# Low parts of a layer's weights kept in DRAM for its second pass, and one subtraction moved from GpSimd to VectorE

## The chip, the cores and the metric

One core of one Trainium2 chip. The metric is the device time of one execution in microseconds (us), the median of three runs. TensorE (PE, with its weight loads as PEld), VectorE (DVE), ScalarE (ACT), GpSimd (POOL) and SyncE (SP, which issues the DMAs here) each run their own in-order queue of instructions and wait for each other by semaphores.

## The reference, cut to what matters

Two layers over 1024 tokens of width 1024. Layer 0 is gated linear attention; layer 1 is sparse attention in which an indexer picks up to 256 keys for each query. What the change touches is in layer 1:

```
h = x @ w_in                       # q: 16 heads x 128, z: 2048, k, v and the indexer's inputs
logits = q . k_sel * ATTN_SCALE    # masked to the chosen keys
probs  = softmax(logits)
o      = probs . v_sel
y      = (o * silu(z)) @ w_out     # 2048 -> 1024
x = layer_norm(ALPHA * x + y);  x = x + (p[i] @ ple_w[i]) * sigmoid(x @ ple_gate_w[i])
```

All of it is float32. The kernel computes each product of two float32 matrices as three matmuls of a reduced type (float32r): each operand a is split into a high part hi = round(a) and a low part lo = a - hi, and hi*hi + hi*lo + lo*hi are summed in PSUM.

## The kernel before

**Two halves.** Each layer runs over 512 tokens, then over the other 512. In layer 1 the first half lies at about 1065 to 1560 us of the span, the second at 1560 to 2134 us, each with a tail (the norm and the gate) behind its 16 heads. Every weight of 128 x 1024 is loaded from DRAM and split anew in each half.

**Weights.** The class `Weights` walks a fixed list `seq` of keys. For each one it loads 512 KB into `wst` (two buffers) by the SP queue, and then makes the parts in four steps: two ACT copies give the halves of `whi` (line 162), two DVE subtractions the halves of `wlo` (line 164); each part has four buffers. `pace` lets a step go when 1.15 us of the kernel's own estimate of TensorE's time have passed, and at most two weights ahead of the one taken; `take` makes what is missing. A `wst` buffer is loaded again when the steps that read it are done. The keys of layer 1 are `dq` (16 blocks of q), `dz` (16 of z), `do` (16 of the output projection), then `p` and `t` for the tail.

**Heads.** `slots()` lays out 17 stretches ("slots"), each with two to four units of weights (q, z or output blocks, 24 matmuls for each weight), and between their matmuls the work of the attention is put in by due times in the same estimate. For head h, `attend` makes:
- A: scores S by PE, minimum and mask into `P` by DVE (line 1357), exp by ACT (line 1377), reciprocal by DVE (line 1381);
- `scaled` and `turned`: the probabilities into `sq` by ACT (line 1365; POOL in the first half, line 1367), and 32 x 32 transposes by DVE (line 1373);
- `store` and `load`: `sq` to DRAM in four DMAs of 256 KB for each group of four key blocks, and back in another order as `PT`, 1 MB at a time (lines 1395 and 1405): one load for a head in the first half, two in the second;
- `parts(g)`: the split of `PT`. ACT copies the high part `ph` (line 1422); 0.8 us of the estimate later a subtraction leaves the low part in `PT` (line 1420). There are three groups g for a head in the first half and seven in the second;
- `pv(g)`: o += vT hi, lo times ph and vT hi times the low part, on PE (tiles `o<-ph,vT`, `o<-PT,vT`), between the matmuls of the weights.

In line 1420 the engine is chosen by half and group: DVE for the even groups (0, 2, 4, 6) of the second half, POOL for its odd groups (1, 3, 5) and for all groups of the first half.

The order of instructions on each engine is that in which this Python code emits them; `manual_schedule` keeps it.

Of the kernel before, what the change touches and what calls it, by code (L numbers as in the profile page):

```python
# [10 lines left out]
F32 = mybir.dt.float32  # L11
# [36 lines left out]
class Flow:  # L48


    def __init__(self, nc):
        self.pe = nc.tensor
        self.now, self.n, self.heap, self.pacers = 0.0, 0, [], []
# [18 lines left out]
    def chain(self, *steps):  # L72

        (_, first), rest = steps[0], steps[1:]
        first()
        if rest:
            self.after(rest[0][0], lambda: self.chain((0, rest[0][1]), *rest[1:]))
# [30 lines left out]
    def pace(self):  # L108
        late = []
        while self.heap and self.heap[0][0] <= self.now:  # L110
            self.one(late)
        self.put_back(late)
        for p in self.pacers:
            p(self.now)
# [23 lines left out]
class Weights:  # L138


    def __init__(self, nc, pool, seq):
        self.nc, self.pool, self.seq = nc, pool, seq
        self.nd = self.ns = self.nu = self.part = 0
        self.due = 0.0
        self.staged, self.parts = {}, {}

    def pace(self, now):
        if now >= self.due and self.step():
# [2 lines left out]
    def step(self):  # L151
        if self.ns >= min(self.nu + 2, len(self.seq)):
            return False
        n, i = self.ns, self.part
        if i == 0:
            self.loads(n + 1)
            self.parts[n] = tuple(self.pool.tile([128, 1024], F32R, tag=t, name=t, bufs=4) for t in ("whi", "wlo"))
        st = self.staged[n]
        hi, lo = self.parts[n]
        c = slice((i % 2) * 512, (i % 2) * 512 + 512)  # L160
        if i < 2:
            self.nc.scalar.activation(hi[:, c], st[:, c], AF.Copy)  # L162
        else:
            self.nc.vector.tensor_sub(lo[:, c], st[:, c], hi[:, c].bitcast(F32))  # L164
        self.part = (i + 1) % 4
        if i == 3:
            self.staged.pop(n)
            self.ns += 1
            self.loads(self.ns + 2)
        return True  # L170
# [42 lines left out]
def trunk_kernel(ctx, tc, x_tok, x_T, p_T, pos, freq, g_q, g_k, g_v, g_z, g_a, g_a2, g_ba, g_gn, g_o,  # L213
                 d_q, d_k, d_v, d_z, d_qi, d_ki, d_o, ln_gb, ple_c, gate_c, out):
    nc = tc.nc
    act, dve, pool = nc.scalar, nc.vector, nc.gpsimd
# [4 lines left out]
    wp = ctx.enter_context(tc.tile_pool(name="wp", bufs=1))  # L221
    xp = ctx.enter_context(tc.tile_pool(name="xp", bufs=1))
    dp = ctx.enter_context(tc.tile_pool(name="dp", bufs=1, space=bass.MemoryType.DRAM))
# [10 lines left out]
    seq = []  # L234
# [7 lines left out]
    def tail_keys(layer):  # L242
        return ([(("p", layer, c), ple_c[layer, c]) for c in range(2)]
                + [(("t", layer, b), gate_c[layer, b]) for b in range(NK)])
# [46 lines left out]
    for half in range(NH):  # L291
# [1 line left out]
            for u in units:  # L293
                seq += unit_keys(u)
        seq += tail_keys(1)
    W = Weights(nc, wp, seq)
    bg, bg2 = Background(), Background()
    fl.pacers += [W.pace, bg.pace, bg2.pace]

# [40 lines left out]
    def pbank():  # L340
        return psum[0].tile([128, 512], F32, tag="pb", name="pb", bufs=psum[1])
# [15 lines left out]
    class XT:  # L357


        def __init__(self):  # L360
            self.t = [None] * NK
# [12 lines left out]
    def fm_block(key, X, evac):  # L374

        hi, lo = W.take(key)
        ps = pbank()
# [119 lines left out]
    def v_phase(u, X):  # L497
        h = u["h"]
        banks = [pbank(), pbank()] + [pp.tile([128, 512], F32, tag="U", name="U", bufs=2) for _ in range(2)]
        for c in range(4):  # L500
            hi, lo = W.take(("v", h, c))
            for t in range(4):
# [188 lines left out]
    def accumulate(parts, U, y, ch, rs=None, norm=None):  # L691

        nb = 2 * len(parts)
        for t in range(4):
            ps = pbank()
            n = 0
            for b in range(nb):
                uh, ul = U(t, b)
                hi, lo = parts[b // 2]
                ws = slice((b % 2) * 512, (b % 2) * 512 + 512)  # L700
                for l, r in ((uh, hi), (uh, lo), (ul, hi)):
                    mm(ps, l, r[:, ws], n == 0, n == 3 * nb - 1)
                    n += 1
                if b < nb - 1:
                    yield
            ys = y[:, t, ch * 512:ch * 512 + 512]
            if rs is not None:
                dve.scalar_tensor_tensor(ys, ps, rs[:, t:t + 1], ys, op0=OP.mult, op1=OP.add)
            else:
                dve.tensor_add(ys, ps, ys)  # L710
            if norm is not None:
                norm(t)
            yield

    def out_phase(u, y, norm=None):
# [4 lines left out]
        for ch in range(2):  # L720
            parts = [W.take(("o", u["h"], ch, 0)), W.take(("o", u["h"], ch, 1))]
            for i, _ in enumerate(accumulate(parts, U, y, ch, u["rs"], norm if ch else None)):
# [39 lines left out]
    def tail(layer, Pt, y, y_done, final, tp, xps, x_alloc, tmp):  # L762
# [15 lines left out]
        for c in range(2):  # L778
            hi, lo = W.take(("p", layer, c))
            for b in range(4):  # L780
# [164 lines left out]
    def index_steps(T, sc, res, kih, kil, ipsum, rtile):  # L945

        n = (T + 1) * 128
        t = T % 4

        def step(i, a, e):  # L950
            def f():
                fl.req(res["q"][i] is not None, "w" in res, "ki" in res)
                e2 = max(e, 256)
                ps = ipsum()
                q = res["q"][i][:, t * 128:t * 128 + 128]
                mm(ps[:, :e2], q, kih[:, a:a + e2], True, False)
                mm(ps[:, :e2], q, kil[:, a:a + e2], False, True)
                r = rtile()
                w = res["w"][:, t, i:i + 1]
                d = sc[:, a:a + e]  # L960

                def add():
                    if i == 0:
                        dve.tensor_scalar(d, r[:, :e], w, None, op0=OP.mult)
                    else:
                        dve.scalar_tensor_tensor(d, r[:, :e], w, d, op0=OP.mult, op1=OP.add)
                    res["n"] = res.get("n", 0) + 1
                    if i == 7 and a + e == n:
                        dve.copy_predicated(sc[:, n - 128:], fmask, negs)
                chain((0, lambda: act.activation(r[:, :e], ps[:, :e], AF.Relu)), (0.8, add))  # L970
            return f

        return fl.ordered([step(i, a, e) for i in range(8) for a, e in cuts(n)])
# [101 lines left out]
    def start_half(half):  # L1075
# [7 lines left out]
        def load(k, n):  # L1083
            nc.sync.dma_start(raw[:, k:k + n], x_T[k:k + n, :, hs].rearrange("k p t -> p k t"))

        def feed():
            load(0, 1)
            W.loads(W.ns + 1)
            load(1, 1)
# [34 lines left out]
    for half in range(NH):  # L1124
# [19 lines left out]
        for h, u in enumerate(units):  # L1144
# [23 lines left out]
            bulk, n = [], 0  # L1168
# [156 lines left out]
    def attend(st, h, half, ap, sq):  # L1325
# [10 lines left out]
        def get(*keys):  # L1336
            fl.req(*(k in st for k in keys))
            return [st[k] for k in keys]
# [70 lines left out]
        def parts(g):  # L1409
            def f():  # L1410
                (j, t0), n = groups[g][0], len(groups[g])
                PT, = get(("PT", h, j // 4))
                fl.req(st["sp"] - st["pv"] < 3)
                st["sp"] += 1
                lo = PT.rearrange("p a (j c) -> p j a c", c=128)[:, j % 4:j % 4 + n, :, 32 * t0:]
                ph = ap.tile([128, HT], F32R, tag="ph", name="ph", bufs=3)
                hi = ph[:, :n * (HT - 128 * t0)].rearrange("p (j a c) -> p j a c", j=n, a=4)

                def second():
                    (dve if half and g % 2 == 0 else pool).tensor_sub(lo, lo.bitcast(F32), hi.bitcast(F32))  # L1420
                    st["parts", h, g] = hi, lo
                chain((0, lambda: act.activation(hi, lo.bitcast(F32), AF.Copy)), (0.8, second))  # L1422
            return f
# [32 lines left out]
        n = range(len(groups))  # L1456
# [75 lines left out]
    for half in range(NH):  # L1532
# [11 lines left out]
        for h, units in enumerate(plan, -1):  # L1544
            start = st["slot"] = fl.now
            dur = sum(len(u[1]) if u[0] == "o" else 1 for u in units) * B + core * (1.0 if h >= 0 else 0.5)
            if h >= 0:
                _, parts, pvs, _, loads = S[h]
# [4 lines left out]
            if h < 15:  # L1553
                first, _, _, stores, loads = S[h + 1]
# [98 lines left out]
```

## Time and profile before

| | |
|---|---|
| median of 3 runs | 2134.95 us (2131.09 to 2135.63) |
| profiled execution | 2135.7 us |
| its span in the trace | 2133.9 us |
| PE busy | 1999.2 us, 94% of the span |
| DVE, ACT, POOL busy | 1539.9 us (72%), 1153.4 us (54%), 326.0 us (15%) |
| TensorE's granted clock, mean | 0.984 of full speed |
| DMA queue q1 | 284.37 MB, 41.5% of 16 engines' span |

Busy time is the union of an engine's instructions; idle time in front of an instruction is put down to the one that released it. The chain of work that ended last follows the last instruction back, at each step to what released it or to the instruction ahead of it on its engine.

### The profile page before, as it was taken

How to read it: one execution, taken by the hardware profiler on the slowest of the kernel's cores; microseconds unless marked ns; L12 is line 12 of the kernel's file. 1: busy time of each engine (PE TensorE's matmuls, PEld its weight loads, DVE VectorE, ACT ScalarE, POOL GpSimd, SP SyncE). 2: the span in 40 equal slices, each digit the busy share in tenths (PEclk: the TensorE clock that was granted, in tenths of full speed). 3: DMA queues.
4: the chain of work that ended last, by engine and by line, in shares of the span. 5: the costliest groups of instructions: out<-in, count | busy, mean ns of one | idle time of the engine just before them, and what ended most of it. 6: DMA issues, size and time to landing. Idle time of an engine off the chain costs nothing.

```text
span 2133.9 us, 26298 instructions
## 1 busy us (share of the span) xinstructions
PE 1999.2 (94%) x8984; PEld 1619.7 (76%) x8984; DVE 1539.9 (72%) x3187; ACT 1153.4 (54%) x2105; POOL 326.0 (15%) x355
## 2 busy tenths in 40 slices
PE   8999999999999999999989899998898889998979
PEld 6788888888788888888867777776686677776767
DVE  5665555676767767667699888786986777777764
ACT  5563535344566353535466677775446655555533
POOL 0100000001011000001012443332112111112110
PEclk9999999999999999999999999999999999999989
DMA  4422222234332222222434555554347665656532
GB/s 141 159 81 79 88 71 89 70 100 143 134 124 70 80 81 83 85 80 84 148 129 151 181 178 169 168 167 153 113 142 231 201 200 195 207 179 212 181 121 97
DMA packets 94197, 286.03 MB, mean 134 GB/s; under 512 B 11120, under 2 KB 11760, under 8 KB 87920
## 3 DMA queue, kind: packets, MB, share of 16 engines
q1 hardware_dynamic: 94064, 284.37, 41.5%
q8 instruction: 70, 1.15, 0.2%
q14 instruction: 63, 0.52, 0.1%
HBM read 220.56 MB, written 63.77 MB: 133 GB/s over the span
## 4 chain that ended last, share of the span: by engine, by line
PE 57%; DVE 20%; ACT 8%; DMA 5%; issue 5%; SPq 1%; POOL 1%; DVEq 0%; POOLq 0%; ACTq 0%
PE pb L58 43%; PE o L58 6%; PE U L58 6%; DVE wlo L164 4%; DVE P L1357 2%; DVE sq L1373 2%; DMA PT<-sqd 1%; PE S L58 1%; DVE rt L853 1%; ACT sq L1365 1%; ACT P L1377 1%; POOL PT L1420 1%; SPq L1395 1%; DMA sqd<-sq 1%; DVE tk L988 1%
## 5 line engine op out<-in xcount | busy, mean ns | idle before, releaser
L58 PE MATMUL pb<-x,whi 128*128 128x512 f32 x2272 | 711.7, 394 | 5.1 <-ACT whi L162 2.4
L58 PEld LDWEIGHTS pb<-x,whi 128*128 128x128 f32 x2272 | 420.1, 189 | 83.6 <-ACT whi L162 3.2
L58 PE MATMUL pb<-x,wlo 128*128 128x512 f32 x1136 | 445.4, 392 | 0.5 <-DVE wlo L164 0.5
L164 DVE TENSOR_TENSOR wlo<-wst,whi 128x512 fp32r<-128x512 f32 x556 | 390.8, 719 | 64.7 <-ACT whi L162 64.3
L162 ACT ACTIVATE whi<-wst 128x512 fp32r<-128x512 f32 x556 | 327.3, 621 | 137.0 <-PE pb L58 28.7
L58 PE MATMUL pb<-whi,u 128*128 128x512 f32 x1024 | 346.0, 398 | 9.5 <-ACT u L352 5.0
L58 PEld LDWEIGHTS pb<-x,wlo 128*128 128x128 f32 x1136 | 214.3, 189 | 48.5 <-DVE wlo L164 2.2
L58 PEld LDWEIGHTS pb<-whi,u 128*128 128x128 f32 x1024 | 195.3, 191 | 50.1 <-ACT u L352 5.8
L58 PE MATMUL pb<-wlo,u 128*128 128x512 f32 x512 | 202.3, 395 | 0.0
L1420 POOL TENSOR_TENSOR PT<-PT,ph 128x512 fp32r<-128x512 f32 (+1 forms) x96 | 131.0, 1371 | 250.3 <-ACT ph L1422 233.1
L58 PE MATMUL o<-ph,vT 128*128 128x512 f32 (+2 forms) x384 | 110.4, 374 | 23.6 <-ACT ph L1422 23.6
L1377 ACT ACTIVATE P<-P,ms 128x128 f32<-128x128 f32 (+7 forms) x128 | 98.6, 770 | 59.3 <-DVE ms L1357 51.5
L58 PE MATMUL S<-kT,q 128*128 128x512 f32 (+2 forms) x576 | 123.1, 344 | 6.3 <-DVE q L344 3.3
L58 PE MATMUL o<-PT,vT 128*128 128x512 f32 x192 | 77.9, 406 | 51.7 <-POOL PT L1420 27.4
L58 PEld LDWEIGHTS S<-kT,q 128*128 128x128 f32 x576 | 100.1, 188 | 26.3 <-DVE q L344 6.1
L58 PEld LDWEIGHTS pb<-wlo,u 128*128 128x128 f32 x512 | 98.0, 191 | 18.4
L1422 ACT ACTIVATE ph<-PT 128x512 fp32r<-128x512 f32 (+1 forms) x160 | 92.6, 598 | 34.2 <-DMA PT<-sqd 11.3
L58 PEld LDWEIGHTS o<-ph,vT 128*128 128x128 f32 x384 | 73.8, 204 | 45.6 <-ACT ph L1422 33.5
L661 ACT ACTIVATE junk<-o 128x512 bf16<-128x512 f32 x32 | 19.1, 597 | 161.1 <-DVE ot L659 151.7
L1373 DVE STREAM_TRANSPOSE sq<-sq 128x128 f32<-128x128 f32 (+7 forms) x128 | 97.0, 764 | 11.0 <-ACT sq L1365 7.2
L1030 ACT ACTIVATE tk<-sc,tki 128x768 f16<-128x768 f32 (+2 forms) x90 | 92.8, 1031 | 22.4 <-DVE tki L1039 21.5
L58 PEld LDWEIGHTS o<-PT,vT 128*128 128x128 f32 x192 | 39.1, 204 | 79.3 <-POOL PT L1420 41.7
(308 smaller groups left out, 3444.9 us busy)
## 6 DMA issues: line engine op xcount, KB each, us to landing
sqd<-sq SPq DMA_DIRECT2D x192, 256.0 KB, 4.4
PT<-sqd SPq DMA_DIRECT2D x48, 1024.0 KB, 6.8
wst<-in_g_v SPq DMA_DIRECT2D x32, 512.0 KB, 3.3
wst<-in_g_z SPq DMA_DIRECT2D x32, 512.0 KB, 3.4
wst<-in_g_o SPq DMA_DIRECT2D x32, 512.0 KB, 3.3
wst<-in_gate_c SPq DMA_DIRECT2D x32, 512.0 KB, 3.5
wst<-in_d_q SPq DMA_DIRECT2D x32, 512.0 KB, 4.6
wst<-in_d_z SPq DMA_DIRECT2D x32, 512.0 KB, 3.5
```

Source lines behind the costliest of these rows:

```text
L58: self.pe.matmul(out, lhsT, rhs, start=start, stop=stop)
L162: self.nc.scalar.activation(hi[:, c], st[:, c], AF.Copy)
L164: self.nc.vector.tensor_sub(lo[:, c], st[:, c], hi[:, c].bitcast(F32))
L853: dve.stream_shuffle(a, x, swap)
L988: dve.tensor_scalar(junk()[:, :n], scs[j], thr_ap, None, op0=op, op1=OP.add, accum_out=cnt[:, j:j + 1])
L1030: act.activation(junk()[:, :n], scs[j], AF.Sign, bias=cand[:, j:j + 1].bitcast(F32), accum_out=cnt[:, j:j + 1])
L1357: dve.tensor_tensor_reduce(P[:, a:a + e], ps[:, :e], bias_t[T][:, a:a + e], op0=OP.add, op1=OP.min, scale=-ATTN_SCALE, scalar=lim, accum_o ...
L1365: act.activation(to, rows, AF.Copy, scale=sm)
L1373: dve.transpose(x, x)
L1377: act.activation(P, P, AF.Exp, scale=-1.0, bias=mx, accum_out=sm)
L1420: (dve if half and g % 2 == 0 else pool).tensor_sub(lo, lo.bitcast(F32), hi.bitcast(F32))
L1422: chain((0, lambda: act.activation(hi, lo.bitcast(F32), AF.Copy)), (0.8, second))
```

## The change

In the first half of layer 1, the low part of each `dq`, `dz` and `do` weight is made as before, and is then also stored to a DRAM tensor `wlos` of its own (512 KB, issued by SP at the second step of the next weight). In the second half these 48 weights have two steps in place of four: the first ACT copy goes out together with a DMA load of the low part from `wlos` into `wlo`, then the second ACT copy; no DVE subtraction. A `wst` buffer is then free after the second copy. The `p` and `t` weights and all of layer 0 are as before.

In line 1420, POOL's odd groups of the second half go to DVE; the first half stays on POOL.

```
-    def __init__(self, nc, pool, seq):
+    def __init__(self, nc, pool, seq, kept, dram):
...
+        self.kept, self.dram, self.low, self.late = kept, dram, {}, None
...
+        key = self.seq[n][0]
...
+        stored = key in self.low
         if i < 2:
             self.nc.scalar.activation(hi[:, c], st[:, c], AF.Copy)
+            if stored and i == 0:
+                self.nc.sync.dma_start(lo.bitcast(F32), self.low[key])
         else:
             self.nc.vector.tensor_sub(lo[:, c], st[:, c], hi[:, c].bitcast(F32))
-        self.part = (i + 1) % 4
-        if i == 3:
+        if i == 1 and self.late:
+            late, self.late = self.late, None
+            self.low[late[0]] = self.dram.tile([128, 1024], F32, name="wlos")
+            self.nc.sync.dma_start(self.low[late[0]], late[1].bitcast(F32))
+        last = i == (1 if stored else 3)
+        self.part = 0 if last else i + 1
+        if last:
+            if key in self.kept and not stored:
+                self.late = key, lo
             self.staged.pop(n)
...
+    kept = {key for key, _ in seq if key[0] in ("dq", "dz", "do")}
+    W = Weights(nc, wp, seq, kept, dp)
...
-                    (dve if half and g % 2 == 0 else pool).tensor_sub(lo, lo.bitcast(F32), hi.bitcast(F32))
+                    (dve if half else pool).tensor_sub(lo, lo.bitcast(F32), hi.bitcast(F32))
```

## Rows read from the trace of the kernel before

**Rows 1.** The page: busy time, and the chain that ended last.
```profile
PE 1999.2 (94%) x8984; PEld 1619.7 (76%) x8984; DVE 1539.9 (72%) x3187; ACT 1153.4 (54%) x2105; POOL 326.0 (15%) x355
...
PE 57%; DVE 20%; ACT 8%; DMA 5%; issue 5%; SPq 1%; POOL 1%; DVEq 0%; POOLq 0%; ACTq 0%
```

**Rows 2.** Busy time by stretch; at each row's end PE clock, DMA share, GB/s.
```profile
1065.00:1470.00 405.00, 371.19 (x1697) 300.17 (x1695) 340.31 (x818) 282.61 (x600) 130.37 (x129) 0.98 0.51 162
...
1560.00:2045.00 485.00, 435.24 (x1928) 347.14 (x1927) 358.00 (x759) 275.83 (x471) 90.30 (x63) 0.97 0.62 196
```

**Rows 3.** Waits of PE, 1560 to 2045 us: total us, times, longest.
```profile
PE o L58 <- DVE PT L1420: 23.7, 21, 2.3
PE o L58 <- ACT ph L1422: 13.3, 10, 4.2
PE o L58 <- POOL PT L1420: 11.2, 12, 2.5
```

**Rows 4.** The chain that ended last, 1560 to 2045 us: shares by line.
```profile
by line: PE pb L58 16.3%; PE o L58 9.5%; issue 7.9%; DVE P L1357 7.2%; DMA PT<-sqd 6.4%; ACT sq L1365 5.7%; DVE wlo L164 5.5%; DVE sq L1373 4.9%; ACT P L1377 3.9%; SPq L1395 3.4%; PE S L58 3.3%; DMA sqd<-sq 3.3%; DVE PT L1420 2.6%; ACT ph L
```

**Rows 5.** Groups by form, 1560 to 2045 us: busy, mean ns, idle before.
```profile
L164 DVE TENSOR_TENSOR wlo<-wst,whi 128x512 fp32r<-128x512 f32 x98 | 71.8, 745 | 6.6 <-ACT whi L162 6.6
...
L1420 POOL TENSOR_TENSOR PT<-PT,ph 128x512 fp32r<-128x512 f32 x31 | 48.9, 1583 | 161.5 <-ACT ph L1422 161.5
...
L1420 DVE TENSOR_TENSOR PT<-PT,ph 128x512 fp32r<-128x512 f32 x62 | 45.4, 739 | 20.2 <-ACT ph L1422 19.9
```

**Rows 6.** Timeline of PE, four waits: start us, us, last the wait.
```profile
1640.77 0.73 PE L58 MATMUL o<-ph,vT 128*128 128x512 f32 x2 [1.06 <-ACT ph L1422]
...
1674.03 0.51 PE L58 MATMUL o<-PT,vT 128*128 128x512 f32 x1 [1.82 <-DVE PT L1420]
...
1731.12 0.50 PE L58 MATMUL o<-PT,vT 128*128 128x512 f32 x1 [2.48 <-POOL PT L1420]
...
1754.85 0.50 PE L58 MATMUL o<-PT,vT 128*128 128x512 f32 x1 [1.33 <-DVE PT L1420]
```

**Rows 7.** Timeline of DVE, and of POOL, ahead of three of these waits.
```profile
1669.98 1.07 DVE L164 TENSOR_TENSOR wlo<-wst,whi 128x512 fp32r<-128x512 f32 x1
...
1672.13 0.64 DVE L164 TENSOR_TENSOR wlo<-wst,whi 128x512 fp32r<-128x512 f32 x1
...
1673.30 1.27 DVE L1420 TENSOR_TENSOR PT<-PT,ph 128x512 fp32r<-128x512 f32 x2
...
1728.06 0.67 DVE L344 TENSOR_TENSOR q<-qf,q 128x512 fp32r<-128x512 f32 x1
...
1727.65 4.38 POOL L1420 TENSOR_TENSOR PT<-PT,ph 128x512 fp32r<-128x512 f32 x2 [3.59 <-ACT ph L1422]
...
1752.49 0.65 DVE L164 TENSOR_TENSOR wlo<-wst,whi 128x512 fp32r<-128x512 f32 x1
```

**Rows 8.** A piece of the chain that ended last: start us, us, what.
```profile
1631.41 0.60 DVE wlo L164
```

**Rows 9.** Busy time by stretch behind a wait; PE clock third from the end.
```profile
1849.00:1852.00 3.00, 3.00 (x8) 2.33 (x9) 0.00 (x0) 0.45 (x1) 0.75 (x1) 0.50 0.93 251
```

**Rows 10.** Waits of the DMA queue (SP), 1560 to 2045 us.
```profile
SPq L175 <- DVE wlo L164: 166.1, 28, 12.6
```

**Rows 11.** DMA issues, 1560 to 2045 us: count, KB each, us to landing.
```profile
PT<-sqd SPq DMA_DIRECT2D x32, 1024.0 KB, 7.0
wst<-in_d_z SPq DMA_DIRECT2D x16, 512.0 KB, 4.1
```

**Rows 12.** Waits of ACT, 1560 to 2045 us.
```profile
ACT whi L162 <- PE pb L58: 13.3, 3, 5.0
...
ACT ph L1422 <- DMA PT<-sqd: 8.9, 1, 8.9
```

**Rows 13.** Issue times of weight loads, 1560 to 2045 us: ns minimum, median, maximum.
```profile
L175 SPq DMA_DIRECT2D wst<-in_d_z x16: 328/333/487, 1562.8 to 1986.7; - x16
```

**Rows 14.** Timeline of ACT at the first half's last head.
```profile
1475.05 1.04 ACT L1422 ACTIVATE ph<-PT 128x512 fp32r<-128x512 f32 x2 [2.42 <-DMA PT<-sqd]
```

More of the change, by code (lines that the diff above doesn't have):

```diff
@@ L295, in trunk_kernel @@
         seq += tail_keys(1)
-    W = Weights(nc, wp, seq)
+    kept = {key for key, _ in seq if key[0] in ("dq", "dz", "do")}
+    W = Weights(nc, wp, seq, kept, dp)
     bg, bg2 = Background(), Background()
```

## The prediction

> **What bounds the kernel now.** The page first: TensorE (PE) is busy for 94% of the span, no other engine for more than 72%, and the chain that ended last lies on PE for 57% and on VectorE (DVE) for 20% [rows 1]. So time is won only where PE stands still or runs at its lower clock. The table by stretch says where: of the 485 us of layer 1's second half (1560 to 2045) PE is busy for 435.2, of the first half's 405 us for 371.2; DVE is busy for 74% of the one and 84% of the other [rows 2]. The changed subtractions run in the second half alone. There PE's waits are 48.2 us, and all three rows belong to the split of the probabilities: 23.7 us for a DVE subtraction of `PT`, 13.3 us for ACT's copy `ph`, 11.2 us for a POOL subtraction [rows 3]. PE waits nowhere for a `wlo`. Yet the chain shows that the 98 `wlo` subtractions are not harmless: 5.5% of 485 us, 26.7 us, of what ended last is `wlo` [rows 4]. They stand in DVE's queue ahead of what PE waits for. To know which, each wait has to be looked at.
>
> **The change part by part.** All sums are made on the profiled execution, 2135.7 us (span 2133.9, 1.8 around it); the median of the runs shown is 2134.95, 0.75 lower.
>
> *DVE's load, second half.* 48 weights lose 2 subtractions each: 96 of the 98 at 745 ns, 71.5 us of DVE. Three odd groups for each of 16 heads come over: 48 at the 739 ns that DVE's own take, 35.5 us (a bound from above, as a third of them have 384 columns and not 512) [rows 5]. Net 36 us of 358 leave DVE. That is load and not time; the time is what PE's waits lose:
>
> (a) Three waits of 1.8 us (heads 1 to 3), one of which is shown at 1674.03 [rows 6]. The subtraction began at 1673.30, and in the 3.3 us ahead of it two `wlo` took 1.07 and 0.64 us [rows 7]. Without them it comes 1.7 us sooner; one subtraction from POOL (0.7) enters the queue. I take 1.0 us each: 3.0.
>
> (b) Three waits of 2.48 us for POOL (heads 4, 8, 12), one at 1731.12 [rows 6]. POOL was slow there: it began at 1727.65, and its two subtractions together took 4.38 us [rows 7], the first until PE's start at 1731.1, 3.4 us, where the mean is 1.58 [rows 5]. On DVE the same work would stand about behind the `q` of 1728.06 [rows 7], and be done at 1728.06 + 0.6 + 0.7, about 1729.3. That is 1.8 us sooner, and at most 2.5; I take 2.0 each: 6.0.
>
> (c) Five waits of 1.33 or 1.44 us for the first group (heads 5, 6, 9, 10, 13), one at 1754.85 [rows 6], each with one `wlo` of 0.6 us close ahead, as at 1752.49 [rows 7]: 0.6 each, 3.0.
>
> (d) Six waits of 1.0 to 1.1 us for `ph` (heads 1, 2, 3, 5, 9, 13), one at 1640.77 [rows 6]. ACT is late there since the minimum, exp and transposes of the next head were late, and the chain through them has a `wlo` of 0.60 us, as at 1631.41 [rows 8]: 0.6 each, 3.6.
>
> (e) POOL's other nine waits, 11.2 - 7.4 = 3.8 us: between nothing (DVE's subtraction is 0.74 us against 1.58, but stands in a longer queue) and all of it. I take 1.0, near the lower end, since DVE's 62 cost PE 0.38 us each now (23.7/62) and POOL's 46 only 0.24 (11.2/46) [rows 3, 5].
>
> (f) The clock. Behind some of these waits the granted clock is 0.50, the 1.2 GHz level, as from 1849 to 1852 [rows 9]; such a stretch of 3.4 us does 1.7 us less. Five follow the waits of (a) and (b). Bounds 0 and 8.5; the waits shrink and don't all go, so I take one: 1.7.
>
> Together 18.3 us. The heads' first waits with no `wlo` ahead stay.
>
> *The stores, first half.* DVE and ACT do what they did. SP issues 48 more DMAs at 0.33 us, 16 us in 405 [rows 13]. A store waits for the same `wlo` for which SP already stands before the next `wst` load, which goes out ahead of it [rows 10] (shown for the second half), so it adds no wait of its own. Behind it on SP are `sqd` stores, `PT` loads and `wst` loads. Its bytes count: 512 KB take about 7.0 - 4.1 = 2.9 us (a load of 1024 KB against one of 512 KB) [rows 11]. What hides that is that `PT` mostly lands before its use. Where it doesn't, PE pays: ACT waited 2.42 us for the last head's [rows 14] and 8.9 us for one in the second half [rows 12]. Bounds: nothing, and 2.9 us for each of 16 loads, 46. I take three loads at half of 2.9, nearer nothing, since two waits among 48 loads are all that the trace has: 4.4 us.
>
> *The loads, second half.* 48 loads of 25 MB raise 196 GB/s to about 248, and the DMA share from 0.62 to about 0.78 [rows 2]. A load goes out at a weight's first step, up to two weights ahead. It waits until PE has let go of the buffer, as the ACT copy beside it does; ACT waited for that three times, 13.3 us in all [rows 12]. SP could wait as long, with `sqd`, `PT` and `wst` DMAs behind it. Bounds 0 and 13.3; nothing taken, as ACT's wait cost PE none. Landing takes 4.1 us [rows 11], and until PE takes the weight there are one or two others to go, 10 us each (48 in 485): hidden. If SP stands for 9 us first, it isn't. `wst` buffers come free sooner, which hurts nobody.
>
> Sum: 18.3 - 4.4 = 13.9 us won, 2135.7 - 13.9 = 2121.8: 2122.
>
> **Rivals.** *The wait only moves.* DVE takes its queue in order, and each of its `PT` subtractions now stands for 0.32 us waiting for ACT's `ph` (19.9/62) [rows 5]; 48 more make 15 us in which DVE does nothing. If the odd groups then cost PE what the even ones cost, 0.38 us, that is 18.2 us for POOL's 11.2, a loss of 7.0. Of (a) to (f) then stay (a), (c) and (d), 9.6, less 4.4 for the stores: 1.8 us lost, 2137.5. For it: DVE waits cost more for each subtraction than POOL's. Against: those are costly because of the `wlo` ahead.
>
> *The way through DRAM becomes the bound (slower).* `PT` loads, SP's stores and the landing of `sqd` are 6.4 + 3.4 + 3.3 = 13.1% of the chain in the second half, 63.5 us [rows 4]. If their 47 us of transfer stretch as the DMA share does (0.78/0.62), that is 12 us more; with SP's 48 issues of 0.33 us on the same path 16 us, and 5 us in the first half: 33 lost against 18.3 won, 15 more: 2150. It decides where a `PT` lands later than it is needed; ACT's single wait of 8.9 us [rows 12] says that most have some us to spare, and the 16 us count only if each issue falls on the path. The Trainium skill, "DMA: Bandwidth & Descriptors", section "Queues, rings and completion order", has the rule that would do this: each DMA engine takes a ring's descriptors in order, so a `PT` load behind a 512 KB transfer waits it out. By that rule each collision costs the 2.9 us taken above, and 2122 becomes this rival's 2150 if nearly every load collides; no row here shows such a collision by itself.
>
> *The low parts come late.* If SP is held and PE waits for `wlo` at the double output units, 2 to 3 us in some four heads: 10 us, 2132. For it only SP's longest wait, 12.6 us [rows 10].
>
> **How the numbers follow.** Less than 0.2% (4.3 us) is about what a measurement of this kernel can't tell from no change. Forecast and its variants that win over 4.3 us: 0.68. The wait moves or the gain is eaten up, within 4.3 us: 0.17. Transfers on the path, slower: 0.15 (late low parts count half in the one and half in the other). The likeliest is 2122. The lower end: all `wlo` on the chain (26.7) and POOL's waits (11.2), less 48 x 0.20 us (DVE's `PT` on the chain, 2.6% of 485 over 62 [rows 4]) = 28, and two clock stretches, 3.4: 31.7 won, 2104. The upper end: a third of the way from 2135.7 to the slow rival, 2140. That leaves 1 in 10 below and 1 in 10 above.
>
> **What would show it.** In the second half: 2 `wlo` on DVE beside 48 loads of `wlo` from DRAM; some 110 `PT` subtractions on DVE at 0.68 to 0.74 us and none on POOL; DVE busy some 36 us less; PE's waits for `PT` down from 34.9 to about 22, for `ph` from 13.3 to about 10, the three waits of 2.48 us gone; clock at 0.97 or 0.98. In the first half: 48 stores, DVE unchanged, the stretch up to 5 us longer. It would be wrong if PE waits for DVE's `PT` exceed 35 us, if waits for `PT<-sqd` pass 20 us, or if PE's row shows a DMA into `wlo`.

## The result, and the profile after

| | before | after |
|---|---|---|
| median | 2135.29 us (4 runs, 2131.09 to 2137.63) | 2104.22 us (4 runs, 2099.89 to 2106.36) |
| profiled execution, its span | 2135.7, 2133.9 us | 2106.36, 2104.1 us |
| ratio to before, 95% interval | | 0.9854 (0.9831 to 0.9877) |

The change makes the kernel 31 us faster, 1.46%. The forecast was 13.9 us, 2122; the measured time stands at the lower end of the range. The direction and the place were right; the forecast gain was less than half of the measured one.

Where the time went shows in one instruction that each half has once, the clearing of `sq` by GpSimd (count, then ns minimum, median and maximum, then the first and the last start). Before:

```profile
L1539 POOL MEMSET sq<- x2: 1798/2665/3532, 1080.2 to 1567.1; 128x2048 f32 x1, 128x4096 f32 x1
```

After:

```profile
L1553 POOL MEMSET sq<- x2: 1797/2660/3524, 1078.6 to 1565.6; 128x2048 f32 x1, 128x4096 f32 x1
```

Layer 1's second half begins 1.5 us sooner; the span ends 29.8 us sooner. So 28.3 us were won behind the start of the second half, and the first half, with its 48 stores, lost nothing in this execution.

The busy time by stretch, after (columns as in [rows 2]):

```profile
1065.00:1470.00 405.00, 370.58 (x1693) 299.71 (x1691) 338.04 (x818) 283.47 (x602) 132.60 (x129) 0.98 0.70 220
...
1560.00:2013.00 453.00, 429.92 (x1918) 346.53 (x1918) 316.47 (x709) 275.60 (x470) 24.11 (x17) 0.97 0.77 264
```

In the second half VectorE is busy for 316.5 us where it was 358.0: 41.5 less, 36 were forecast. The DMA share is 0.77 (0.78 was forecast). The granted clock is the same 0.97 as in [rows 2], but as the mean of two parts that moved apart. Heads 1 to 3 and the heads behind them, before:

```profile
1640.00:1706.00 66.00, 55.43 (x232) 42.95 (x233) 47.46 (x97) 39.67 (x69) 15.23 (x12) 0.92 0.63 194
1706.00:2045.00 339.00, 305.74 (x1366) 244.44 (x1365) 249.17 (x533) 190.08 (x325) 62.62 (x44) 0.99 0.61 195
```

After:

```profile
1637.00:1703.00 66.00, 58.73 (x241) 46.44 (x241) 45.78 (x97) 40.58 (x70) 2.84 (x3) 0.87 0.74 243
1703.00:2013.00 310.00, 299.17 (x1355) 241.06 (x1354) 219.76 (x499) 188.89 (x323) 12.86 (x10) 1.00 0.77 265
```

In heads 1 to 3 the clock fell from 0.92 to 0.87, behind them it rose from 0.99 to 1.00. PE's waits from 1560 to 2013 us, which answer to [rows 3]:

```profile
PE o L58 <- DVE PT L1434: 14.0, 15, 1.8
PE o L58 <- ACT ph L1436: 5.4, 5, 3.7
PE pb L58 <- DMA wlo<-wlos: 3.2, 1, 3.2
```

48.2 us of waits have become 22.6: 25.6 won, where the forecast's items (a) to (e) came to 16.6. The wait for a low part from DRAM, a rival's mechanism and one of the forecast's own signs of being wrong, is there once. VectorE's groups, after:

```profile
L1434 DVE TENSOR_TENSOR PT<-PT,ph 128x512 fp32r<-128x512 f32 (+1 forms) x108 | 68.3, 654 | 23.5 <-ACT ph L1436 23.5
```

All 108 subtractions of `PT` in the stretch are on VectorE. The mean is over two shapes; those of 128 x 512 alone took 671 ns, where VectorE's took 739 before, beside POOL's [rows 5].

The DMAs of the second half (count, KB each, us to landing), after, against [rows 11]:

```profile
PT<-sqd SPq DMA_DIRECT2D x31, 1024.0 KB, 7.6
wlo<-wlos SPq DMA_DIRECT2D x47, 512.0 KB, 7.8
```

`PT` lands 0.6 us later than before; the new loads take 7.8 us, nearly twice what a `wst` load of z took (4.1).

### The profile page after: what moved, and what is told of

It reads as the page before. It is cut to its first block, busy times and chain, and to the rows that moved or that the text cites. A ratio compares the mean times of both kernels' runs of the same rounds, so it can differ in the third digit from the quotient of the medians.

```text
span 2104.1 us, 26226 instructions
## 1 busy us (share of the span) xinstructions
PE 1998.5 (95%) x8984; PEld 1622.8 (77%) x8984; DVE 1496.1 (71%) x3139; ACT 1153.6 (55%) x2105; POOL 258.6 (12%) x307
## 3 DMA queue, kind: packets, MB, share of 16 engines
q8 instruction: 70, 1.15, 0.2%
## 4 chain that ended last, share of the span: by engine, by line
PE 65%; DVE 14%; ACT 8%; DMA 6%; issue 5%; POOL 1%; SPq 1%; DVEq 0%; POOLq 0%; ACTq 0%
PE pb L58 48%; PE o L58 7%; PE U L58 6%; DVE wlo L170 2%; PE S L58 2%; ACT sq L1379 2%; DVE P L1371 1%; DMA wlo<-wlos 1%; ACT P L1391 1%; DVE sq L1387 1%; DMA PT<-sqd 1%; DVE rt L867 1%; DVE sc L980 1%; DVE tk L1002 1%; SPq L1409 1%
## 5 line engine op out<-in xcount | busy, mean ns | idle before, releaser
L170 DVE TENSOR_TENSOR wlo<-wst,whi 128x512 fp32r<-128x512 f32 x460 | 317.0, 706 | 57.1 <-ACT whi L166 55.4
L1436 ACT ACTIVATE ph<-PT 128x512 fp32r<-128x512 f32 (+1 forms) x160 | 93.8, 599 | 44.4 <-DMA PT<-sqd 16.6
L58 PE MATMUL pb<-whi,x 128*128 128x512 f32 x256 | 89.2, 408 | 9.5 <-ACT whi L166 6.2
L866 POOL TENSOR_TENSOR rt<-qf,tab 32x512 f32<-32x512 f32 x32 | 41.8, 1306 | 439.0 <-ACT qf L1288 433.1
```

Of the source, the lines that this page charges most:

```text
L58: self.pe.matmul(out, lhsT, rhs, start=start, stop=stop)
L866: pool.tensor_mul(b, x, c)
```

## The experiments

All ran beside runs of the kernel before on the same chip; each ratio is to those.

| run | what it is | median us | ratio to before, 95% interval |
|---|---|---|---|
| e1_weights_only | low parts from DRAM, odd groups on POOL | 2099.52 | 0.9841 (0.9824 to 0.9858) |
| e2_engine_only | weights as before, all groups on VectorE | 2125.36 | 0.9965 (0.9952 to 0.9978) |
| e3_stores_only | stores, never read | 2136.51 | 1.0011 (0.9999 to 1.0023) |
| e4_more_traffic | changed kernel, 48 more copies | 2104.70 | 0.9861 (0.9841 to 0.9880) |
| e8_time_back | e1, with a transpose for each removed subtraction | 2124.07 | 0.9948 (0.9934 to 0.9963) |
| e9_sub_back | e1, with a subtraction for each removed one | 2137.73 | 1.0015 (1.0006 to 1.0025) |
| e5_low_by_pool | low parts made by POOL, no DRAM | 2126.56 | 0.9959 (0.9945 to 0.9972) |
| e6_pool_early_heads | changed kernel, odd groups of heads 0 to 3 on POOL | 2100.34 | 0.9843 (0.9829 to 0.9857) |
| e7_pool_late_heads | changed kernel, odd groups of heads 4 to 15 on POOL | 2102.91 | 0.9853 (0.9838 to 0.9868) |
| e10_last_by_dve | e1, last three output weights made again | 2099.96 | 0.9837 (0.9822 to 0.9853) |

**The two parts of the change, each alone.** First the weights alone, against the changed kernel:

```
-                    (dve if half else pool).tensor_sub(lo, lo.bitcast(F32), hi.bitcast(F32))
+                    (dve if half and g % 2 == 0 else pool).tensor_sub(lo, lo.bitcast(F32), hi.bitcast(F32))
```

> Low parts from DRAM in the second half; the odd groups stay on POOL. Theory Q (VectorE's queue: the time won is mostly that of the weights' subtractions standing ahead of what TensorE waits for): 16 to 22 us faster than before, about 2116; VectorE is busy some 75 us less in the second half, TensorE's waits for VectorE's PT fall from 23.7 to under 12 us, waits for POOL's PT stay at 8 to 11. Theory P (GpSimd: its subtractions are slow and slow VectorE's): under 12 us faster, 2124 or more, and the waits for POOL's PT stay at 11 us.

34 us won: by the medians more than the whole change, though the two intervals overlap. Both theories were too low, and both expected more waits for POOL. PE's waits, 1560 to 2006 us, weights alone:

```profile
PE o L58 <- DVE PT L1434: 10.0, 13, 1.3
PE o L58 <- ACT ph L1436: 5.3, 5, 3.6
PE pb L58 <- DMA wlo<-wlos: 4.5, 3, 3.4
PE o L58 <- POOL PT L1434: 4.2, 8, 0.6
```

The waits for POOL fell from 11.2 to 4.2 us, the longest from 2.5 to 0.6, though POOL does what it did before. The forecast's item (b), 6 us, was booked to the move to VectorE; the weights alone bring it. VectorE's own subtractions of `PT` did not get shorter beside POOL's: 62 of them take 807 ns, where they took 739 [rows 5].

```profile
L1434 DVE TENSOR_TENSOR PT<-PT,ph 128x512 fp32r<-128x512 f32 x62 | 49.4, 807 | 22.4 <-ACT ph L1436 22.2
```

The other part alone, in the kernel before:

```
-                    (dve if half and g % 2 == 0 else pool).tensor_sub(lo, lo.bitcast(F32), hi.bitcast(F32))
+                    (dve if half else pool).tensor_sub(lo, lo.bitcast(F32), hi.bitcast(F32))
```

> All groups of the second half on VectorE, the weights made as before. Theory Q: VectorE is 36 us busier, its queue longer; the 11.2 us of POOL waits turn into VectorE waits: between 3 us faster and 10 us slower than before, 2132 to 2145. Theory P: at least 8 us faster, 2127 or less.

0.35% faster, 7.5 us: theory P's side for this one. PE's waits and VectorE's two subtractions, 1560 to 2036 us:

```profile
PE o L58 <- DVE PT L1420: 30.8, 25, 2.4
PE o L58 <- ACT ph L1422: 12.4, 8, 4.2
```

```profile
L164 DVE TENSOR_TENSOR wlo<-wst,whi 128x512 fp32r<-128x512 f32 x96 | 63.8, 676 | 6.2 <-ACT whi L162 6.2
L1420 DVE TENSOR_TENSOR PT<-PT,ph 128x512 fp32r<-128x512 f32 x93 | 60.9, 671 | 12.2 <-ACT ph L1422 12.1
```

POOL's 11.2 us went and VectorE's 23.7 rose to 30.8. That VectorE was not simply 36 us busier shows in the second view: with POOL's subtractions gone, `wlo` takes 676 ns in place of 745 and `PT` 671 in place of 739 [rows 5]. VectorE's busy time rose by 8.9 us.

The two parts do not add up: 0.35% and 1.59% alone, 1.46% together. So the question became what in the removed subtractions had cost so much.

**Time or collisions.** Two kernels give VectorE back an instruction for each removed subtraction, and differ in its operands alone. Both are e1 with

```
+        elif stored:
+            self.nc.vector.transpose(st[:, c], st[:, c])                               # e8
+            self.nc.vector.tensor_sub(st[:, c], st[:, c], hi[:, c].bitcast(F32))       # e9
...
-        last = i == (1 if stored else 3)
+        last = i == 3
```

where the one or the other line stands. The used buffer is overwritten; the low part that PE uses still comes from DRAM. In both, a weight has four steps again and `wst` comes free only behind VectorE's instruction, as before the change.

> Weights from DRAM, odd groups on POOL, and at the two steps where the second half's subtractions of the weights stood, VectorE transposes the weight's used buffer in place instead (one operand, about the same 0.7 us, a result that nobody reads): its time is given back, its two-operand traffic is not. Theory Q (the time in VectorE's queue is what was won): most of the 34 us are lost again, 2122 to 2136, and TensorE's waits for VectorE's PT are back at 20 us or more. Theory C (what was won is that two-operand subtractions of VectorE and GpSimd no longer collide): 2108 or less, and the POOL subtraction's mean stays at 1.3 us. In either case, if the three waits of 2.48 us for POOL came from collisions with the weights' subtractions, they stay away.

> As e8_time_back, but at the two steps VectorE subtracts the weight's high part from the used buffer in place (two operands, as the removed subtraction was) instead of transposing it; the low part that is used still comes from DRAM. It differs from e8 in nothing but the number of SBUF operands. If collisions of two-operand subtractions with GpSimd's are the other part of the gain: 6 to 10 us slower than e8, 2130 to 2136, the POOL subtraction's mean back at 1.45 us, waits for POOL's PT back at 10 us or more, with the three of some 2.5 us. If they are not: 2122 to 2126 as e8, and the rest of the gain came from the loads or the buffers.

With the subtraction back, all of the gain is gone (1.0015; e9 does on VectorE and POOL what the kernel before does, so the 0.15%, some 3 us, is what the stores and loads cost by themselves). With the transpose, a gain of 0.52% stays, the time that theory Q forecast. e9 is 14 us slower than e8, more than the 6 to 10 expected. VectorE's dummy and POOL's subtraction, e8 (1560 to 2035 us), the second with ns minimum, median, maximum:

```profile
L170 DVE STREAM_TRANSPOSE wst<-wst 128x512 f32<-128x512 f32 x96 | 64.9, 688 | 6.9 <-ACT whi L166 6.9
```

```profile
L1436 POOL TENSOR_TENSOR PT<-PT,ph x46: 1009/1293/1577, 1615.9 to 2027.3; 128x512 fp32r<-128x512 f32 x31, 128x384 fp32r<-128x384 f32 x15
```

The same, e9 (1560 to 2045 us):

```profile
L170 DVE TENSOR_TENSOR wst<-wst,whi 128x512 f32<-128x512 f32 x96 | 70.6, 748 | 6.3 <-ACT whi L166 6.3
```

```profile
L1436 POOL TENSOR_TENSOR PT<-PT,ph x46: 1001/1296/3411, 1609.8 to 2037.9; 128x512 fp32r<-128x512 f32 x31, 128x384 fp32r<-128x384 f32 x15
```

And PE's waits, e8 and then e9:

```profile
PE o L58 <- DVE PT L1436: 18.4, 16, 2.3
...
PE o L58 <- POOL PT L1436: 4.3, 10, 0.6
```

```profile
PE o L58 <- DVE PT L1436: 19.1, 18, 2.3
...
PE o L58 <- POOL PT L1436: 11.0, 11, 2.5
```

One operand more, and POOL's slowest subtraction takes 3.41 us again, VectorE's dummy 748 ns for 688, and the POOL waits are back at 11.0 us. The subtraction is not the longer instruction by itself: without POOL's beside it, it took 676 ns (e2). So the gain of the weights alone has two parts. From e9 to e8 it is the collisions of VectorE's two-operand subtractions with POOL's: (1.0015 - 0.9948) x 2134 = 14 us, some 4 either way by the intervals. From e8 to e1 it is the instruction's time in VectorE's queue, together with the later release of `wst` and the two more steps, which no run separates from it: (0.9948 - 0.9841) x 2134 = 23 us, some 5 either way. Of PE's waits between e8 and e1, those for VectorE's `PT` and ACT's `ph` fall by 13.8 us (18.4 and 10.7 to 10.0 and 5.3), those for a low part from DRAM by 2.2 (6.7 to 4.5), and PE waits for no `whi` in either. A part of both steps is the clock's: it was 0.96 in the stretch of e9, 0.98 in that of e8 and 0.99 in that of e1. The Trainium skill, "SBUF — State Buffer", section "Who interferes with whom", says that a VectorE instruction with two SBUF inputs contends with a GpSimd instruction that reads SBUF, and one with at most one input outside the two-port modes does not; these two runs agree, with POOL's 3.41 against 1.58 us.

**The low parts made by POOL instead.** The other way to relieve VectorE, without DRAM (the kernel before with all groups on VectorE):

```
-            self.nc.vector.tensor_sub(lo[:, c], st[:, c], hi[:, c].bitcast(F32))
+            again = self.seq[n][0] in dict(self.seq[:n]) and self.seq[n][0][0] in ("dq", "dz", "do")
+            (self.nc.gpsimd if again else self.nc.vector).tensor_sub(lo[:, c], st[:, c], hi[:, c].bitcast(F32))
```

> No DRAM copies: in the second half GpSimd makes the low parts of the same 48 weights, VectorE all groups of the probabilities. VectorE does what it does in the changed kernel. Theory Q: 2100 to 2112, near the changed kernel's 2104. Theory C: GpSimd's 96 subtractions collide with VectorE's; its PT subtractions, 0.65 us in the changed kernel, grow to 0.75 us or more, and the time is 2116 or more.

Its groups, 1560 to 2036 us:

```profile
L165 POOL TENSOR_TENSOR wlo<-wst,whi 128x512 fp32r<-128x512 f32 x96 | 139.2, 1461 | 250.7 <-ACT whi L162 184.2 <-DVE x L808 51.1 <-DMA sqd<-sq 14.5
...
L1421 DVE TENSOR_TENSOR PT<-PT,ph 128x512 fp32r<-128x512 f32 x93 | 74.7, 820 | 12.8 <-ACT ph L1423 12.8
```

The busy time in the same stretch:

```profile
1560.00:2036.00 476.00, 436.45 (x1929) 346.02 (x1927) 352.38 (x709) 275.14 (x470) 162.40 (x113) 0.97 0.62 200
```

Theory C: VectorE's subtractions of `PT` take 820 ns, a fifth more than without POOL's, its 709 instructions 352.4 us where the changed kernel's 709 take 316.5, and the time is that of the engine's move alone (2125.36). PE waits for none of POOL's low parts, so it is not that they come late. Moving two-operand work to GpSimd gives little back here; taking it away does.

**The stores, and the room in the DMA queue.** Stores without a reader (the changed kernel with `stored = False`, each key stored once, the odd groups on POOL):

```
-        stored = key in self.low
+        stored = False
...
-            if key in self.kept and not stored:
+            if key in self.kept and key not in self.low:
```

> The 48 low parts are stored in the first half and never read; all else as before. The forecast's term: 4.4 us slower than before. If the stores are hidden: within 2 us of before although the PT loads of the first half land some 3 us later (8.7 for 5.3 us). If they are not and the changed kernel's first half only hid them: 5 to 10 us slower.

Between nothing and 5 us (-0.2 to 4.9 by the interval): the forecast's 4.4 stands inside, and so does a hidden store. In its trace the first half's `PT` loads land after 8.4 us:

```profile
wlos<-wlo SPq DMA_DIRECT2D x47, 512.0 KB, 6.8
PT<-sqd SPq DMA_DIRECT2D x16, 1024.0 KB, 8.4
```

Before:

```profile
PT<-sqd SPq DMA_DIRECT2D x16, 1024.0 KB, 5.3
```

That is 3.1 us later, close to the 2.9 that the forecast took for 512 KB ahead of a load, and most of it is hidden.

More traffic in the second half:

```
             if stored and i == 0:
                 self.nc.sync.dma_start(lo.bitcast(F32), self.low[key])
+                self.nc.sync.dma_start(self.dram.tile([128, 1024], F32, name="copy"), self.low[key])
```

> The changed kernel, and in its second half each of the 48 low parts is also copied from DRAM to another DRAM tensor that nobody reads (24 MB more read and written, 48 more issues on SP). If the way through DRAM has room in the second half: at most 4 us slower than the changed kernel, 2104 to 2108. If the DRAM round trip is close behind TensorE: 12 us slower or more, 2116 or above, with TensorE waiting for wlo or for the copies of PT that wait for their load.

No cost that can be measured, with the DMA share at 0.89 (last but one) in 1560 to 2017 us:

```profile
1560.00:2017.00 457.00, 433.87 (x1942) 349.60 (x1940) 320.84 (x715) 277.83 (x473) 24.09 (x17) 0.97 0.89 316
```

The slower rival, the way through DRAM as the bound, is ruled out for this amount of traffic and for 48 more copies of 512 KB.

**Which heads want POOL.** The weights alone were no slower than with the engine's move. To see where the move might cost, the changed kernel with POOL in some heads:

```
-                    (dve if half else pool).tensor_sub(lo, lo.bitcast(F32), hi.bitcast(F32))
+                    (dve if half and (g % 2 == 0 or h > 3) else pool).tensor_sub(lo, lo.bitcast(F32), hi.bitcast(F32))   # e6
+                    (dve if half and (g % 2 == 0 or h < 4) else pool).tensor_sub(lo, lo.bitcast(F32), hi.bitcast(F32))   # e7
```

> The changed kernel, but the odd groups of heads 0 to 3 on POOL. If the 5 us that separate the changed kernel from the weights alone lie in the first heads (two transposes stand ahead of the first odd group on VectorE, a wait of 1.76 us, and the clock falls to half in heads 1 to 3): 2095 to 2100. If they come from VectorE's longer queue everywhere: 2102 to 2105.

> The converse: odd groups of heads 4 to 15 on POOL, those of heads 0 to 3 on VectorE. If the first heads are the cause: 2104 to 2108, with the clock at half in heads 1 to 3. If VectorE's longer queue everywhere is: 2099 to 2102.

Neither decides it by its time: e6's median lies just above the range for the first heads, e7's between its two ranges, and the intervals of e6, e7, e1 and the changed kernel overlap, so the order of the times is not shown. The traces say more. VectorE in the changed kernel, head 1:

```profile
1638.35 2.22 DVE L1387 STREAM_TRANSPOSE sq<-sq 128x896 f32<-128x896 f32 x2
1640.51 0.64 DVE L1434 TENSOR_TENSOR PT<-PT,ph 128x512 fp32r<-128x512 f32 x1
```

The first odd group stands behind two transposes; PE waits 1.75 us for it, where with the weights alone it waits 0.50 for POOL and 1.04 for the next even group. And the stretch of heads 1 to 3 by busy time, which took 66 us at a clock of 0.87 in the changed kernel (the row above). First e1 and e6, with POOL in these heads, in one fence each, then e7, with VectorE:

```profile
1637.00:1697.00 60.00, 53.31 (x248) 41.87 (x248) 43.53 (x90) 40.50 (x70) 14.65 (x12) 1.00 0.78 259
```

```profile
1636.00:1696.00 60.00, 53.44 (x249) 42.01 (x250) 43.45 (x91) 40.30 (x70) 14.38 (x12) 1.00 0.79 259
```

```profile
1637.00:1697.00 60.00, 53.72 (x226) 42.95 (x227) 42.37 (x93) 36.64 (x63) 2.56 (x2) 0.89 0.79 258
```

Much the same matmuls take 66 us at a mean granted clock of 0.87 and 60 us at 1.00; e7 had got through 226 of them in its 60 us, at 0.89. From the end of PE's first wait in head 1 to that in head 6, e1 and e6 take 125.8 and 126.1 us, e7 and the changed kernel 131.1 and 133.1; from there to the last head's wait, e1 takes 249.7 and the changed kernel 249.9. So in the profiled executions the move costs 5 to 7 us, all of it by head 6. The clocks of all executions agree: of the eight of these two kernels, the four with a mean granted clock of 0.987 or 0.988 took 2096.79 to 2100.38 us, the four at 0.984 or 0.985 took 2102.45 to 2106.36; three of the first four are e1's, three of the others the changed kernel's. Ahead of each fall PE had stood some 2.4 us for `ph` and `PT`; with the weights alone it stood 2.2 us, in four pieces, and the clock stayed. What makes the difference these rows don't show.

**The late low part.** In e1 PE waits 3.35 us at 2002.94 for a low part whose load SP issued behind a `PT` load.

```
-    kept = {key for key, _ in seq if key[0] in ("dq", "dz", "do")}
+    kept = {key for key, _ in seq if key[0] in ("dq", "dz", "do")} - {("do", 6, 1), ("do", 7, 0), ("do", 7, 1)}
```

> The weights alone, without the last three output weights (do 6,1; 7,0; 7,1), which VectorE makes again in the second half: TensorE's wait of 3.35 us for a low part from DRAM near the end goes, 3 us faster than the weights alone, 2095 to 2098. If the late PT load behind it sets the end of that stretch anyway: no change, 2098 to 2101, and the wait for ACT's ph there grows from 5.7 us by what was won.

No change. PE near the end of e10's heads:

```profile
2005.14 0.73 PE L58 MATMUL o<-ph,vT 128*128 128x512 f32 x2 [1.96 <-ACT ph L1436]
2014.42 1.22 PE L58 MATMUL o<-ph,vT 128*128 128x512 f32 x2 [5.22 <-ACT ph L1436]
```

The 3.35 us wait is gone and PE stands 1.96 us for `ph` instead: what comes behind was no sooner there. The 5.7 us wait for `ph`, which was to grow, is 5.22. Best of all versions by the median, though not apart from its neighbours, is e1; it beats the kernel before by 34 us.

## Why the prediction was right in its direction and wrong in its size

**What bounds the kernel: right.** Time was won where PE stood for the split of the probabilities, in the second half, by 48.2 - 22.6 = 25.6 of the 28.3 us (1.1 us of short waits for `q` went too).

**The load: right.** 36 us of VectorE were forecast, 41.5 measured. The subtractions of `PT` are 68.3 us where the forecast had 45.4 + 35.5 = 80.9: without POOL's beside them they are shorter than the 739 ns taken.

**The step that failed** is the pricing of what PE's waits lose, items (a) to (f): it counted for each wait for `PT` only the `wlo` that stands close ahead in VectorE's queue, and put "the heads' first waits with no `wlo` ahead" at nothing. It had 16.6 us for the waits; 25.6 were won. By the PE timelines of the two kernels:

| item | forecast us | measured us |
|---|---|---|
| (a) VectorE waits of heads 1 to 3 | 3.0 | 0.2: 1.8 each before, 1.75 after, now for the first odd group behind two transposes |
| (b) three waits of 2.48 for POOL | 6.0 | 7.4: all gone |
| (c) five first waits with a `wlo` ahead | 3.0 | 4.8: 1.33 fell to 0.12, 1.44 to 0.84 |
| (d) six waits for `ph` | 3.6 | 4.9: 6.3 fell to 1.3 |
| (e) POOL's other waits | 1.0 | 3.8: all gone |
| first waits with no `wlo` ahead (six, heads 4, 7, 8, 11, 12, 14) | 0 | 3.8: 8.9 fell to 5.2 |
| (f) clock | 1.7 | about 0, of two parts (estimated from the rows above): heads 1 to 3 lost 66 x 0.08 = 5.3 us before and 66 x 0.13 = 8.6 after, the heads behind them 339 x 0.01 = 3.4 before and none after |
| stores | -4.4 | about -3 (e3; 0 to -5), in the changed kernel's own trace nothing |

Head 7 shows how a wait with no `wlo` close ahead got shorter. PE's wait before, after, and in e8:

```profile
1812.50 0.50 PE L58 MATMUL o<-PT,vT 128*128 128x512 f32 x1 [2.25 <-DVE PT L1420]
```

```profile
1799.98 0.50 PE L58 MATMUL o<-PT,vT 128*128 128x512 f32 x1 [1.27 <-DVE PT L1434]
```

```profile
1805.86 0.50 PE L58 MATMUL o<-PT,vT 128*128 128x512 f32 x1 [2.25 <-DVE PT L1436]
```

Two `wlo` subtractions stood 11 and 8 us ahead of it, each in front of a result for which ACT waited, the minimum and the reciprocal (VectorE, then ACT):

```profile
1801.10 0.69 DVE L164 TENSOR_TENSOR wlo<-wst,whi 128x512 fp32r<-128x512 f32 x1
...
1804.66 0.69 DVE L164 TENSOR_TENSOR wlo<-wst,whi 128x512 fp32r<-128x512 f32 x1
```

```profile
1803.20 1.05 ACT L1377 ACTIVATE P<-P,ms 128x896 f32<-128x896 f32 x1 [1.56 <-DVE ms L1357]
...
1805.46 0.94 ACT L1365 ACTIVATE sq<-P,ms 128x768 f32<-128x768 f32 x1 [0.40 <-DVE ms L1381]
```

After, ACT waits 0.95 us for the minimum:

```profile
1791.19 1.05 ACT L1391 ACTIVATE P<-P,ms 128x896 f32<-128x896 f32 x1 [0.95 <-DVE ms L1371]
```

For the reciprocal it doesn't wait: 0.61 + 0.40 = 1.01 us sooner, and PE's wait is 0.98 shorter. VectorE had even been idle in between, for ACT. The forecast followed this way through ACT for `ph` in item (d), and not for the first waits. e8 confirms it: with a transpose in the place of each subtraction, the first waits of heads 5 to 7, 9 to 11, 13 and 14 are back at 1.15 to 2.27 us, each within 0.02 of the kernel before; in e2, which only moved POOL's work, they never left. In (c), three of the five lost 1.2 us and two the 0.6 forecast.

By the spans, 29.8 us were won and 13.9 forecast. The 15.9 between are 9.0 of PE's waits, 4.4 of stores that cost nothing in this execution, 1.5 from ahead of the second half and 2.7 behind its start outside the three rows of waits, less the 1.7 of clock.

**A second miss in the same step:** the 2.48 us waits for POOL were read as a slow POOL, whose work is better done elsewhere. They were collisions with a run of VectorE's instructions that had the `wlo` subtractions in it: without these (e1), or with one-operand transposes in their place (e8), the three waits are gone, with two-operand ones (e9) they are back at 2.47 and 2.48. The row was in the forecast, a POOL subtraction of 3.4 us [rows 7], and its gain was booked to the move. The move alone (e2) only turns the three into waits of 1.18 to 1.20 us for VectorE.

**The rivals.** The wait only moves: it did so in heads 1 to 3 alone. The way through DRAM: `PT` lands 0.6 us later in the second half, without a cost, and e4 doubles the new traffic for nothing. The low parts come late: once, 3.2 us, at the very end; e10 shows for e1 that there it costs nothing. In e1, e8 and e9 PE waits for them three or four times, 4.5 to 6.7 us. The chain that ended last, after, 1560 to 2013 us:

```profile
by line: PE pb L58 28.6%; PE o L58 16.1%; ACT sq L1379 7.1%; issue 6.8%; DMA wlo<-wlos 6.1%; ACT P L1391 4.3%; DVE P L1371 4.2%; PE S L58 3.9%; DMA PT<-sqd 2.8%; DVE sq L1387 2.6%; DVE PT L1434 2.6%; SPq L1409 2.5%; DVE rt L867 1.8%; DMA xs
```

It has 6.1% on these loads, more than the 5.5% of `wlo` in [rows 4] that the forecast took for its lower end, and PE waited for them for 3.2 us: a share of the chain is not yet time that can be won.

**Still open:** why, with the low parts from DRAM, the clock falls in heads 1 to 3 when VectorE has the odd groups there and not when POOL has them (before the change it fell with POOL's too, to 0.92), and whether it does so in every execution (the medians of the changed kernel and of e1 are 4.7 us apart, their intervals overlap); and how the 23 us from e8 to e1 divide between VectorE's time and the later release of `wst`.

## What to carry to other kernels

Taking work from a queue that feeds the bounding engine can be worth more than the instructions just ahead of its waits, since a delay also travels through the other engines: put the time back with a harmless instruction of the same length to see what the queue alone costs, before the gain is ascribed to anything else. Where an engine's instruction takes more than twice its median, look for what ran beside it first; here removing the neighbour gave 34 us (e1) and moving the victim 7.5 (e2). A mean over a stretch can hide two parts that moved apart, as the clock's 0.97 did. And test the parts of a change one by one: here one part did all of it, by the medians.

## What the hardware showed that was not expected

- VectorE's two-operand subtraction and GpSimd's, side by side, lengthen each other: GpSimd's to 3.41 us at most where it is 1.58 at most beside one-operand transposes; VectorE's from 671 ns on the mean (e2, none on GpSimd) to 739 before, 807 in e1, where the weights' subtractions were gone and GpSimd's 48 stayed, and 820 in e5, where GpSimd made 96 low parts.
- The DMA queue took 0.89 of 16 engines' time and 316 GB/s for 457 us, with 96 more issues than the kernel before in that half; the second 48 had no measurable cost (2104.70 against 2104.22 us).
- A 512 KB load of low parts took 7.8 us to land, where a weight's load of z, of the same size, had taken 4.1 us [rows 11], and PE waited for one once (in e8 four times).
